# Stacked gate products in a recurrence, and attention scores in two steps per pair of heads

## The chip, the cores and the metric

The kernel runs on one core of one Trainium2 chip. The time is the device time of that core for one execution, in microseconds (us); a kernel's time is the median of its runs. TensorE is called PE in the profile, and its loading of the stationary operand PEld; DVE is VectorE, ACT is ScalarE, POOL is GpSimd, and SP is the engine that issues the DMAs.

## What is computed

One step of a 2-layer encoder, for a prompt of 512 tokens and a sample of 32 tokens, both with the same weights. Width is 1024. A layer is three parallel branches, a gated merge and a layer norm:

```python
def layer(x, pe, ...):                       # shortened
    u = x @ w_in                             # 1024 -> 8192 columns
    qa, ka, va, za, qb, kb, vb, zb, xr, zc, ga, gb, gc = split_cols(u)
    ya = band_attention(qa, ka, va, rel_table) * silu(za)      # 8 heads of 64
    yb = group_norm_heads(retention(rope(qb), rope(kb), vb)) * silu(zb)
    yc = rg_lru(xr, ...) * silu(zc)
    merged = sum(sigmoid(g) * (y @ w_branch[i]) for i, (g, y) in ...)
    r = ALPHA * x + merged @ w_out
    r = r + sigmoid(r @ w_ple_gate) * (pe @ w_ple)
    return layer_norm(r, ln_gain, ln_bias)

def rg_lru(xr, s_conv, s_lru, ...):          # shortened; w = 512 in 8 blocks of 64
    xc = conv_b + sum(xpad[:, j:j + t] * conv_w[j] for j in range(4))
    xb = xc.reshape(b, t, 8, 64)
    r = sigmoid(einsum('btni,nij->btnj', xb, w_gate_a) + b_gate_a)
    ig = sigmoid(einsum('btni,nij->btnj', xb, w_gate_x) + b_gate_x)
    log_a = -8.0 * r * softplus(-lru_lambda)
    a = exp(log_a);  bx = sqrt(-expm1(2 * log_a)) * ig * xc
    h = associative_scan(a, bx)              # h[t] = a[t] * h[t - 1] + bx[t]
```

The prompt's attention is over up to 512 keys in chunks of 64: a chunk of queries sees its own chunk and all before it. A learned bias per head is added to the scores ahead of the softmax. The sample's 32 queries see 256 cached keys and their own 32.

## The kernel before

**Layout.** Activations lie with features on the 128 partitions and the 544 tokens (512 and 32) along the free dimension. An fp32 product is made of three products of fp32r parts: each operand is cast to a high part (`hilo`, line 264, on ACT, for activations; `split`, line 211, on ACT, for weights), and DVE subtracts it to give the low part (lines 265 and 212). Products are high by high, high by low, and low by high.

**Blocks.** The weights are cut into blocks of 128 x 128. `block()` (line 256) makes six matmuls for one: three products, each for 288 and 256 tokens. Weights stream from DRAM in chunks of eight blocks (`load`, line 203, issued on SP), and are split four blocks at a time. Nearly all of PE's work is these blocks, and the rest of each layer is put between them.

**Order.** The order of the program is the order on every engine. It is written by hand: after each block `tick()` runs the jobs that are due. A job is a Python generator; what it yields is the number of ticks until it goes on, mostly an entry of the table `PACE`. A tick is thus one block, six matmuls.

**The recurrence's gates.** `lru_tile(t)` handles 128 of the 512 channels, two of the eight 64 x 64 gate blocks: convolution (lines 510 to 512), eight ticks (`lt1`), then cast and split of `xc` (547 columns: 512, three of padding, 32), five ticks (`lt2`), then two groups of six matmuls (line 522), three ticks (`lt3`) after each. A group is one gate for all 128 channels: its weight is block-diagonal, with two 64 x 64 blocks and zeros elsewhere, three products in two pieces of 274 columns, into two PSUM buffers (`sc` and `pv`). Three sigmoids on ACT follow a group (lines 525 to 527), and POOL multiplies the input gate by `xc` (lines 529, 530). `lru_job` then makes the coefficients and the scans (lines 555, 556).

**The attention.** For each pair of heads `attn_job` starts three steps of `attn_step`, eight ticks apart: query tiles 0 and 1 (128 and 256 keys), tile 2 (384), tile 3 (512). A step makes the scores of both heads (line 407, three products each, the two heads on the two halves of PE's rows), a softmax (lines 357 to 364, on DVE and ACT) and, at `at1` + `at1` + `at2` = 8 ticks after the scores, transposes of the probabilities (line 423) with their copies. The products with the values (line 441) wait in a list until the first transposes of the next pair's first step, where `flush()` makes them. `sample_job` does the same for the 32 sample tokens.

**PSUM** has eight banks: `mm` (two buffers of two banks) for blocks, `sc` (two), `tp` (one), `pv` (one). A `tmp` buffer is one of 14 in SBUF of 128 x 544 or a little more.

## Time and profile before

| | |
|---|---|
| time, median of 3 runs | 1309.05 us (1308.57 to 1309.22) |
| the profiled execution's own time | 1308.99 us |
| its span on the core | 1307.2 us |
| instructions in the span | 25,090 |
| mean granted clock of TensorE | 0.997 |
| PE, weight loads | busy 99% and 96% of the span |
| DVE, ACT, POOL | busy 55%, 42%, 13% of the span |

How to read the rows that follow in the prediction. A row of the timeline is: start in us from the span's start, duration in us, engine, line of the kernel, operation, output and inputs by the program's names, partitions x elements and type, number of instructions; then, in brackets, the idle time of the engine ahead of it and what ended it. PE rows overlap, since matmuls are pipelined: the distance of their starts is what one costs. A row of the waits is: engine, tile and line that waited, what released it, the sum of waiting in us, the count, the longest. In a row of the windows stand, for each stretch, its length, the busy time of PE, PEld, DVE, ACT, POOL and SP's DMA queue with counts, the granted clock, the share of the DMA engines and their GB/s.

### The profile page before, as it was taken

The numbers are of one execution on the slowest core, as the hardware profiler recorded it, in microseconds if no ns is written. First come the engines' busy times: TensorE is split into PE (matmuls) and PEld (weight loads), VectorE is DVE, ScalarE is ACT, GpSimd is POOL, SyncE is SP. The second block draws the span as 40 slices with busy tenths as digits, with TensorE's granted clock in tenths as the row PEclk, the third lists the DMA queues.
The fourth block names the chain that finished last, engine by engine and source line by source line (L and its number), as shares of the span: only waits on it lengthen the run. The fifth ranks groups of instructions, "written<-read, shape, count | busy, mean of one in ns | idle before, by whom it ended". The sixth has DMA issues, their size and how long they took to land.

```text
span 1307.2 us, 25090 instructions
## 1 busy us (share of the span) xinstructions
PE 1290.2 (99%) x10552; PEld 1255.8 (96%) x10552; DVE 719.6 (55%) x1273; ACT 547.0 (42%) x1083; POOL 176.3 (13%) x158
## 2 busy tenths in 40 slices
PE   9999999999999999999999999999999999999996
PEld 9999889999999999999989998999999999999996
DVE  5666663563754443455584756626637534434567
ACT  6665544323632233323277655443235322332231
POOL 0210121410101101000032102125001011010000
PEclk9999999999999999999999999999999999999998
DMA  7333522321222222434132335222212222224231
GB/s 285 132 131 98 174 66 83 96 92 51 96 81 82 98 80 82 165 101 143 65 112 72 130 99 166 74 83 89 87 62 81 98 81 89 90 82 166 81 114 69
DMA packets 44609, 134.80 MB, mean 103 GB/s; under 512 B 9488, under 2 KB 11792, under 8 KB 42704
## 3 DMA queue, kind: packets, MB, share of 16 engines
q1 hardware_dynamic: 44496, 133.20, 30.6%
q8 instruction: 83, 1.36, 0.5%
q14 instruction: 30, 0.25, 0.1%
HBM read 117.02 MB, written 11.70 MB: 98 GB/s over the span
## 4 chain that ended last, share of the span: by engine, by line
PE 95%; DVE 3%; DMA 1%; ACT 1%; issue 0%; SPq 0%; POOL 0%; DVEq 0%
PE mm L256 84%; PE sc L407 2%; PE pv L441 1%; PE tp L423 1%; PE tp L334 1%; DMA raw<-in_W 1%; PE sc L667 1%; PE pv L690 1%; PE pv L522 0%; DVE r L819 0%; PE sc L522 0%; DVE xl L265 0%; PE sc L750 0%; PE sc L603 0%; PE pv L685 0%; PE sc L494 0%
## 5 line engine op out<-in xcount | busy, mean ns | idle before, releaser
L256 PE MATMUL mm<-xh,wh 128*128 128x288 f32 x2144 | 455.5, 294 | 0.4 <-ACT xrp L900 0.4
L256 PE MATMUL mm<-xh,wl 128*128 128x288 f32 x2144 | 444.2, 288 | 0.0
L256 PE MATMUL mm<-xl,wh 128*128 128x288 f32 x2144 | 442.8, 288 | 0.0
L212 DVE TENSOR_TENSOR wl<-raw,wh 128x512 fp32r<-128x512 f32 (+1 forms) x354 | 262.6, 760 | 282.3 <-ACT wh L211 277.2
L256 PEld LDWEIGHTS mm<-xh,wh 128*128 128x128 f32 x2144 | 328.4, 189 | 10.8 <-issue 7.5
L256 PEld LDWEIGHTS mm<-xl,wh 128*128 128x128 f32 x2144 | 328.8, 188 | 0.0
L256 PEld LDWEIGHTS mm<-xh,wl 128*128 128x128 f32 x2144 | 328.6, 188 | 0.0
L211 ACT CAST wh<-raw 128x512 fp32r<-128x512 f32 (+1 forms) x354 | 208.2, 614 | 36.0 <-PE mm L256 30.8
L922 ACT ACTIVATE sg<-mm 128x544 f32<-128x544 f32 x48 | 30.0, 625 | 154.0 <-PE mm L256 154.0
L934 POOL TENSOR_TENSOR m<-m,sg 128x544 f32<-128x544 f32 x30 | 46.8, 1561 | 316.7 <-DVE sg L932 316.7
L359 ACT ACTIVATE sx<-sx,sst 128x128 f32<-128x128 f32 (+4 forms) x68 | 38.0, 559 | 67.1 <-DVE sst L357 60.2
L256 PE MATMUL mm<-xh,held 128*128 128x288 f32 (+1 forms) x320 | 64.1, 292 | 0.3 <-ACT ple L942 0.3
L256 PE MATMUL mm<-mh,wh 128*128 128x288 f32 (+1 forms) x256 | 53.0, 288 | 0.0
L256 PE MATMUL mm<-mh,wl 128*128 128x288 f32 (+1 forms) x256 | 53.0, 288 | 0.0
L256 PE MATMUL mm<-ml,wh 128*128 128x288 f32 (+1 forms) x256 | 52.8, 287 | 0.0
L256 PEld LDWEIGHTS mm<-xh,held 128*128 128x128 f32 x320 | 51.3, 188 | 0.6 <-ACT ple L942 0.5
L256 PE MATMUL mm<-xl,held 128*128 128x288 f32 (+1 forms) x160 | 46.4, 290 | 0.6 <-DVE xl L265 0.6
L264 ACT CAST xh<-r 128x544 fp32r<-128x544 f32 (+2 forms) x32 | 17.0, 532 | 68.3 <-DVE r L952 64.1
L932 DVE TENSOR_TENSOR sg<-mm,sg 128x544 f32<-128x544 f32 x32 | 23.2, 725 | 37.0 <-PE mm L256 37.0
L913 ACT ACTIVATE z<-mm 128x544 f32<-128x544 f32 x24 | 15.0, 626 | 60.6 <-PE mm L256 60.5
L571 POOL TENSOR_TENSOR swap<-swap,cst 128x544 f32<-128x544 f32 x16 | 24.9, 1554 | 108.3 <-DMA swap<-QB 32.1
L256 PEld LDWEIGHTS mm<-mh,wh 128*128 128x128 f32 x256 | 39.4, 189 | 0.0
(251 smaller groups left out, 1783.4 us busy)
## 6 DMA issues: line engine op xcount, KB each, us to landing
raw<-in_W SPq DMA_DIRECT2D x189, 512.0 KB, 3.3
pled<-ple SPq DMA_DIRECT2D x4, 1088.0 KB, 9.8
ple<-pled SPq DMA_DIRECT2D x4, 1088.0 KB, 7.0
bias<-in_RB SPq DMA_DIRECT2D x16, 256.0 KB, 3.7
x<-in_xT SPq DMA_DIRECT2D x4, 544.0 KB, 9.5
o_v<-VA SPq DMA_DIRECT2D x2, 1088.0 KB, 4.6
o_k<-KT SPq DMA_DIRECT2D x2, 1088.0 KB, 5.1
swap<-KB SPq DMA_DIRECT2D x32, 68.0 KB, 2.0
```

Source lines behind the costliest of these rows:

```text
L211: S.copy(h[:, k:k + step], t)
L212: V.tensor_tensor(lo[:, k:k + step], t, h[:, k:k + step].bitcast(F32), SUB)
L256: T.matmul(ps[:, MM0 + a:MM0 + b], lhsT=w[:, n % 4, :], rhs=x[:, a:b], start=first and i == 0, stop=last and i == 2)
L264: S.copy(h, src)
L334: T.transpose(tp[:rows, t * 128:(t + 1) * 128], src[:, t, c0:c0 + rows], ident)
L359: S.activation(x, x, AF.Exp, bias=s[:, 0:1], scale=-1.0, accum_out=s[:, 1:2])
L407: T.matmul(scs[j][:, o:o + n], lhsT=q_[r, p, i * 128:i * 128 + 128], rhs=k_[r, p, :n], start=k == 0, stop=k == 2)
L571: G.tensor_tensor(sw, sw, cst[:, C_SIN:C_SIN + N], MUL)
L913: S.activation(z, pv, AF.Sigmoid)
L922: S.activation(sg, pv, AF.Sigmoid)
L932: V.tensor_tensor(sg, pv, sg, MUL)
L934: (V if kind == "bB" and t == 7 else G).tensor_tensor(m, m, sg, ADD)
```

## The change

Two parts of the kernel are changed, with the paces that place them.

**Gate products.** After the split of `xc`, four DMAs within SBUF build two tiles `xs[0]` and `xs[1]` of 128 rows: the high part of one gate block's 64 channels in one half of the rows, and the low part of the same channels in the other. The weight tile holds the `a` and the `x` matrix of that block side by side, and the same again below. A group is now one gate block: two products instead of three (high weights by the stacked rows, low weights by the stacked rows), and the result has gate `a` on 64 partitions and gate `x` on the other 64. So a tile has two groups of four matmuls. The first group uses the two `sc` buffers, the second `pv` and `tp`. Four sigmoids on 64 partitions follow each group, of 274 and 273 columns. POOL multiplies all 547 columns in one instruction. The tiles `lru_r`, `lru_i`, `lru_a` are 547 wide. The stacked rows also add the product of low weights by low activations to the sum. `lt0`, the delay ahead of a tile's job, is now 2, 11, 12, 13 for the four tiles (before: 2, and 8 for tile 1).

**Scores.** A pair of heads has a wide step (query tiles 3 and 1: 512 and 256 keys, in `sc`, `sc`, `tp`, `pv`) and a narrow one (tiles 2 and 0: 384 and 128 keys side by side in the two `sc` buffers); 11 ticks follow the first, 13 the second. The list of value products is emptied after the first transposes of the wide step. `sample_job` loads its bias later, makes the scores of both halves in one go, and all its transposes in one go into two `sc` buffers. The copies of VA from PSUM go from ACT to DVE.

```diff
@@ -69,8 +69,8 @@
 PACE = {
     "turn": 2, "spill": 16, "tk": 1, "bc0": 3, "bc1": 4, "x": 5,
-    "va0": 5, "va": 3, "step": 8, "attn_end": 9, "at1": 3, "at2": 2, "at3": 3, "sample": 11, "sa1": 4, "sa2": 4,
-    "sa3": 3, "lt0": 2, "lt00": 8, "lt1": 8, "lt2": 5, "lt3": 3, "lru0": 3, "lru1": 3, "lru2": 1, "lru3": 3,
+    "va0": 5, "va": 3, "step": (11, 13), "attn_end": 3, "at1": 3, "at2": 2, "at3": 3, "sample": 14, "sa1": 4, "sa2": 4,
+    "sa3": 3, "lt0": (2, 11, 12, 13), "lt1": 8, "lt2": 5, "lt3": 3, "lru0": 2, "lru1": 2, "lru2": 1, "lru3": 2,
     "rope1": 6, "rope2": 5, "rope3": 3, "tok": 2, "kv": 4, "mu": 2, "mu2": 2, "dec": 2, "rs": 2, "y1": 3,
     "y2": 1, "y3": 1, "gn": 8, "gn1": 2, "gn2": 6, "gn3": 2}
@@ -377,11 +378,11 @@
                 for j in range(2):
                     G.memset(env["bias", p, j][0:64, 448:512], NEG)
-                for qs in ((0, 1), (2,), (3,)):
-                    if qs[0] == 2 and p < 3:
+                for n, qs in enumerate(((3, 1), (2, 0))):
+                    if n and p < 3:
                         bias_loads(p + 1)
                     add(attn_step(p, qs))
-                    yield PACE["step"]
+                    yield PACE["step"][n]
             yield PACE["attn_end"]
             flush()
@@ -393,22 +394,31 @@
         def attn_step(p, qs):
             QTh, QTl, KTh, KTl = (env[k] for k in ("QTh", "QTl", "KTh", "KTl"))
-            scs, xs, todo = [psum("sc") for _ in range(2)], [], []
-            o = 0
+
+            wide = qs[0] == 3
+            scs, xs = [psum("sc") for _ in range(2)], [tmp("sx", (128, 512)) for _ in range(2)]
+            at_ = {(qs[0], j): (scs[j], xs[j], 0) for j in range(2)}
+            if wide:
+                x = tmp("sx", (128, 512))
+                at_.update({(qs[1], j): (psum(("tp", "pv")[j]), x, 256 * j) for j in range(2)})
+            else:
+                at_.update({(qs[1], j): (scs[j], xs[j], 128 * (qs[0] + 1)) for j in range(2)})
             now = [], []
 
-            for j in range(2):
-                xs.append(tmp("sx", (128, 512)))
             for i in qs:
                 n = (i + 1) * 128
...
                     for j in range(2):
                         r = slice(64 * j, 64 * j + 64)
-                        T.matmul(scs[j][:, o:o + n], lhsT=q_[r, p, i * 128:i * 128 + 128], rhs=k_[r, p, :n],
+                        sc, x, o = at_[i, j]
+                        o *= not wide
+                        T.matmul(sc[:, o:o + n], lhsT=q_[r, p, i * 128:i * 128 + 128], rhs=k_[r, p, :n],
                                  start=k == 0, stop=k == 2)
                 for j in range(2):
-                    now[j].append((xs[j][:, o:o + n], scs[j][:, o:o + n], env["bias", p, j][:, 512 - n:]))
-                o += n
+                    sc, x, o = at_[i, j]
+                    c = 0 if wide else o
+                    now[j].append((x[:, o:o + n], sc[:, c:c + n], env["bias", p, j][:, 512 - n:]))
+            todo = []
             for j in range(2):
                 for a in todo:
@@ -417,21 +427,21 @@
                 norm(*a)
             yield PACE["at2"]
-            for j in range(2):
+            for x in xs + ([at_[1, 0][1]] if wide else []):
                 tp = psum("tp")
-                for c in range(0, o, 128):
-                    T.transpose(tp[:, c:c + 128], xs[j][:, c:c + 128], ident)
-
-                if j == 0 and qs[0] == 0:
+                mine = sorted((o, i, j) for (i, j), (_, y, o) in at_.items() if y is x)
+                end = mine[-1][0] + 128 * (mine[-1][1] + 1)
+                for c in range(0, end, 128):
+                    T.transpose(tp[:, c:c + 128], x[:, c:c + 128], ident)
+
+                if wide and x is xs[0]:
                     flush()
-                c = 0
-                for i in qs:
+                for c, i, j in mine:
                     copy("p%d" % j)(env["PT"][j][:, :i + 1, i * 128:i * 128 + 128],
                                     tp[:, c:c + 128 * (i + 1)].rearrange("p (a b) -> p a b", b=128))
-                    c += 128 * (i + 1)
+                if not wide and x is xs[1]:
+                    env["pvs"].append(lambda: attn_pv(p))
                 yield PACE["at3"]
-            if qs[-1] == 3:
-                env["pvs"].append(lambda: attn_pv(p))
 
         def attn_pv(p):
@@ -453,37 +463,39 @@
         def sample_job():
             ks, vc = sample_loads()
+            while "ya" not in env:
+                yield 2
+            yield PACE["sample"]
             sb = [tmp("sb", (128, PAST + NS)) for _ in range(2)]
             for h in range(8):
                 Q.dma_start(out=sb[h % 2][32 * (h // 2):32 * (h // 2) + 32],
                             in_=RB[l, h, 0:NS, 128:128 + PAST + NS])
-            while "ya" not in env:
-                yield 2
-            yield PACE["sample"]
+            yield 12
             xs = []
+            scs = [psum("sc") for _ in range(2)]
             for j in range(2):
                 r = slice(64 * j, 64 * j + 64)
-                sc = psum("sc")
                 for p in range(4):
-                    T.matmul(sc[32 * p:32 * p + 32, :PAST + NS], lhsT=env["qs"][r, p], rhs=ks[r, p],
+                    T.matmul(scs[j][32 * p:32 * p + 32, :PAST + NS], lhsT=env["qs"][r, p], rhs=ks[r, p],
                              tile_position=(64 * j, 32 * p))
+            for j, sc in enumerate(scs):
                 xs.append(exps(tmp("sx", (128, PAST + NS)), sc[:, :PAST + NS], sb[j]))
                 yield PACE["sa1"]
...
                 norm(*x)
             yield PACE["sa2"]
...
@@ -503,7 +516,7 @@
         def lru_tile(t):
             if t == 0:
-                env["lru"] = [sl("lru_r"), sl("lru_i"), sl("lru_a")]
+                env["lru"] = [sl(k, shape=(128, 4, W547)) for k in ("lru_r", "lru_i", "lru_a")]
...
@@ -511,23 +524,28 @@
                 V.scalar_tensor_tensor(xc, xrp[:, t, j:j + W547], pcol(P_CW + 4 * j, t), xc, MUL, ADD)
             yield PACE["lt1"]
-            xch, xcl = (tp_.tile([128, W547], F32R, tag="tmp", name="xch") for _ in range(2))
+
+            xch, xcl, *xs = (tp_.tile([128, W547], F32R, tag="tmp", name="xhl") for _ in range(4))
+            rows = slice(0, 64), slice(64, 128)
             hilo(xch, xcl, xc)
+            for b in range(2):
+                Q.dma_start(out=xs[b][rows[b]].bitcast(F32), in_=xch[rows[b]].bitcast(F32))
+                Q.dma_start(out=xs[b][rows[1 - b]].bitcast(F32), in_=xcl[rows[b]].bitcast(F32))
             yield PACE["lt2"]
-            for g in range(2):
-                w, lo = ([parts[(l * NB + AT["wg"] + g * 4 + t) // 4][i][:, t] for i in range(2)])
-                ps = psum("sc"), psum("pv")
-                for i, (wg, x) in enumerate(((w, xch), (w, xcl), (lo, xch))):
+            for b in range(2):
+                n = l * NB + AT["wg"] + 2 * t + b
+                ps = [psum(k) for k in (("pv", "tp") if b else ("sc", "sc"))]
+                for i in range(2):
                     for p_, c0 in ((ps[0], 0), (ps[1], W547 - 274)):
-                        T.matmul(p_[:, :274], lhsT=wg, rhs=x[:, c0:c0 + 274], start=i == 0, stop=i == 2)
-                d = (I if g else R)[:, t]
-                b_ = pcol(P_BX if g else P_BA, t)
-                S.activation(d[:, :274], ps[0][:, :274], AF.Sigmoid, bias=b_)
-                S.activation(d[:, 274:NP], ps[1][:, 1:NP - 273], AF.Sigmoid, bias=b_)
-                S.activation(d[:, NP:], ps[1][:, 274 - NS:274], AF.Sigmoid, bias=b_)
+                        T.matmul(p_[:, :274], lhsT=parts[n // 4][i][:, n % 4], rhs=xs[b][:, c0:c0 + 274],
+                                 start=i == 0, stop=i == 1)
+
+                for d, r, b_ in ((R, rows[b], P_BA), (I, rows[1 - b], P_BXS)):
+                    b_ = pcol(b_, t)[r]
+                    S.activation(d[rows[b], t, :274], ps[0][r, :274], AF.Sigmoid, bias=b_)
+                    S.activation(d[rows[b], t, 274:], ps[1][r, 1:274], AF.Sigmoid, bias=b_)
                 yield PACE["lt3"]
-            G.tensor_tensor(I[:, t, :NP], I[:, t, :NP], xc[:, :NP], MUL)
-            G.tensor_tensor(I[:, t, NP:], I[:, t, NP:], xc[:, NP + 3:], MUL)
+            G.tensor_tensor(I[:, t], I[:, t], xc, MUL)
             if t == 3:
                 env["gates"] = True
@@ -901,7 +919,7 @@
                     Q.dma_start(out=o_cv[l, :, :, 0:3], in_=xrp[:, :, NP:NP + 3])
                     Q.dma_start(out=o_cv[l, :, :, 3:6], in_=xrp[:, :, NP + NS + 3:NP + NS + 6])
-                add(lru_tile(t), PACE["lt00"] if t == 1 else PACE["lt0"])
+                add(lru_tile(t), PACE["lt0"][t])
@@ -1085,10 +1103,8 @@ (on the host, before the launch)
         for n, (kind, t, k) in enumerate(BLOCKS):
             if kind == "wg":
-                W[l, n // 8, :, n % 8] = 0
-                for b in range(2):
-                    r = slice(64 * b, 64 * b + 64)
-                    W[l, n // 8, r, n % 8, r] = g["w_gate_x" if k // 4 else "w_gate_a"][l, 2 * (k % 4) + b]
+                ax = [g[a][l, k] for a in ("w_gate_a", "w_gate_x")]
+                W[l, n // 8, :, n % 8] = np.tile(np.concatenate(ax[::-1] if k % 2 else ax, 1), (2, 1))
```

The places in the program where this moves work, on the engines that wait or are waited for there:

ACT, layer 0 of before, from the last group of tile 0 (gate `x`) to the first group of tile 1; `par_91` are the layer's biases and other columns, `xrp` is the padded input of the convolution, and the convolution's step is tile 2's:

```order
L211 CAST wh<-raw 128x512
L525 ACTIVATE lru_i<-sc,par_91 128x274
L526 ACTIVATE lru_i<-pv,par_91 128x238
L527 ACTIVATE lru_i<-pv,par_91 128x32
L264 CAST xch<-xc 128x547
L510 ACTIVATE xc<-xrp,par_91 128x547
L211 CAST wh<-raw 128x512
L525 ACTIVATE lru_r<-sc,par_91 128x274
```

The same stretch in the changed kernel:

```order
L212 CAST wh<-raw 128x512
L545 ACTIVATE lru_r<-pv,par_91 64x274
L546 ACTIVATE lru_r<-tp,par_91 64x273
L545 ACTIVATE lru_i<-pv,par_91 64x274
L546 ACTIVATE lru_i<-tp,par_91 64x273
L265 CAST xhl<-xc 128x547
L523 ACTIVATE xc<-xrp,par_91 128x547
L212 CAST wh<-raw 128x512
L545 ACTIVATE lru_r<-sc,par_91 64x274
```

The cast of a tile stands directly behind the sigmoids of the last group of the tile before, in both. There are four of them, on 64 partitions, where there were three on 128.

SP, the same stage of before, where only weights, two small outputs and the second chunk of `ple` are issued:

```order
L850 DMA pled<-ple 128x2176
L203 DMA raw<-in_W 128x1024 x2
L902 DMA o_cv<-xrp 512x1x3
L903 DMA o_cv<-xrp 512x1x3
L203 DMA raw<-in_W 128x1024 x4
```

SP after; `xhl<-xhl` is one copy of 64 rows into `xs`:

```order
L868 DMA pled<-ple 128x2176
L204 DMA raw<-in_W 128x1024
L532 DMA xhl<-xhl 64x547
L533 DMA xhl<-xhl 64x547
L532 DMA xhl<-xhl 64x547
L533 DMA xhl<-xhl 64x547
L204 DMA raw<-in_W 128x1024
L920 DMA o_cv<-xrp 512x1x3
L921 DMA o_cv<-xrp 512x1x3
L532 DMA xhl<-xhl 64x547
```

Four copies a tile are added to SP's queue, sixteen a layer, between the loads of weights.

DVE, layer 0, the softmax of the first attention step of before, from its first reductions to its first normalisation (`sst` holds the row sums; ISA is the reduction of line 357, which also adds the bias):

```order
L357 ISA sx,sst<-sc,bias 128x128
L357 ISA sst 128x1
L357 ISA sx,sst<-sc,bias 128x256
L357 ISA sst 128x1
L555 SCALAR_TENSOR_TENSOR lru_i<-lru_a,lru_r 128x512
L556 SCALAR_TENSOR_TENSOR lru_i<-lru_a,par_91,lru_r 128x32
L212 TENSOR_TENSOR wl<-raw,wh 128x512
L363 RECIPROCAL sst<-sst 128x1
L364 TENSOR_SCALAR sx<-sx,sst 128x128
```

The same after (the scans are lines 573 and 574, the reduction is line 358):

```order
L358 ISA sx,sst<-sc,bias 128x512
L358 ISA sst 128x1
L358 ISA sx,sst<-tp,bias 128x256
L358 ISA sst 128x1
L573 SCALAR_TENSOR_TENSOR lru_i<-lru_a,lru_r 128x512
L574 SCALAR_TENSOR_TENSOR lru_i<-lru_a,par_91,lru_r 128x32
L213 TENSOR_TENSOR wl<-raw,wh 128x512
L573 SCALAR_TENSOR_TENSOR lru_i<-lru_a,lru_r 128x512
L574 SCALAR_TENSOR_TENSOR lru_i<-lru_a,par_91,lru_r 128x32
L364 RECIPROCAL sst<-sst 128x1
L365 TENSOR_SCALAR sx<-sx,sst 128x512
```

Between the step's first reductions and its first normalisation there are now two scans where there was one (a further pair stands ahead of the reductions), and the reductions are over 512 and 256 keys, in the place of 128 and 256.

28 lines of the change are left out of this document (15 added, 13 removed).

## Prediction

> **What bounds the kernel now.** I read the page first (busy shares, slices, chain), then the waits of the engines, then the timeline of the two stages that change.
>
> ```profile
> PE 1290.2 (99%) x10552; PEld 1255.8 (96%) x10552; DVE 719.6 (55%) x1273; ACT 547.0 (42%) x1083; POOL 176.3 (13%) x158
> PEclk9999999999999999999999999999999999999998
> PE 95%; DVE 3%; DMA 1%; ACT 1%; issue 0%; SPq 0%; POOL 0%; DVEq 0%
> ```
> ```profile
> PE tp L750 <- DVE r L968: 2.0, 2, 1.4
> SPq L203 <- DVE wl L212: 787.4, 139, 11.0
> ```
> PE is the chain for 95% of the span, and its longest entry in the list of waits is 2.0 us in all. So PE is a queue that hardly ever stops: what is taken out of it is gained in full, and every wait put into it is lost in full, since nothing later in the program has room to make it good. Everything below is therefore priced on PE alone; the other engines count only where PE waits for them. The second row says that the weight loads stand on SP until a buffer is free (787.4 us of waiting): they are early, and more work on SP costs nothing until that is used up.
>
> **The recurrence's products.** A tile now has two groups of six products; it gets two groups of four. The order has 32 matmuls of 274 columns fewer, and nothing else of PE's changes here.
>
> ```profile
> 37.91 0.64 ACT L211 CAST wh<-raw 128x512 fp32r<-128x512 f32 x1
> ...
> 39.39 0.69 DVE L212 TENSOR_TENSOR wl<-raw,wh 128x512 fp32r<-128x512 f32 x1
> 40.26 0.72 DVE L265 TENSOR_TENSOR xch<-xc,xch 128x547 fp32r<-128x547 f32 x1
> 41.56 0.19 PEld L522 LDWEIGHTS sc<-xch,held 128*128 128x128 f32 x1
> 41.68 0.29 PE L522 MATMUL sc<-xch,held 128*128 128x274 f32 x1
> ...
> 42.31 0.29 PE L522 MATMUL pv<-xch,held 128*128 128x274 f32 x1
> 42.51 0.49 ACT L525 ACTIVATE lru_r<-sc,par 128x274 f32<-128x274 f32 x1 [0.67 <-PE sc L522]
> 42.90 0.45 ACT L526 ACTIVATE lru_r<-pv,par 128x238 f32<-128x238 f32 x1
> ...
> 46.44 0.66 ACT L264 CAST xch<-xc 128x547 fp32r<-128x547 f32 x1
> 46.46 1.30 POOL L529 TENSOR_TENSOR lru_i<-lru_i,xc 128x512 f32<-128x512 f32 x1 [46.02 <-ACT lru_i L526]
> 47.13 1.21 DVE L265 TENSOR_TENSOR xch<-xc,xch 128x547 fp32r<-128x547 f32 x1 [1.06 <-ACT xch L264]
> ```
> ```profile
> 42.60 2.27 PE mm L256 x18
> ```
> ```profile
>   ACT lru_r L527: 0.6, 2
> ```
> Six products start between 41.68 and 42.31, one every 0.126 us; the blocks between them have the same pitch (2.27 over 18). 32 x 0.126 = 4.0 us gained. Line 522's matmuls also waited 0.6 us for the sigmoids of the group before (last row, from that line's own view); with four PSUM buffers for two groups that goes: 0.6 gained.
>
> **The transfers** are what I expect to decide. Before, the operands of a group were ready when DVE had split them (line 265). Now four DMAs follow the split, and PE still comes five ticks after it (a tick is one block, six matmuls, 0.755 us). What a small copy within SBUF costs:
>
> ```profile
> DMA to landing us min/median/max: 1.9/2.0/3.7
> L568 SPq DMA_DIRECT2D swap<-KB x16: 582/588/591, 146.0 to 824.1; - x16
> ```
> ```profile
> o_y<-tk SPq DMA_DIRECT2D x6, 256.0 KB, 2.1
> ```
> The rope's swaps (68 KB) land 2.0 us after their issue, the 256 KB of o_y 2.1; a copy of 64 rows has 140 KB, so I take 2.1, and 0.1 for the two semaphores (issue and wake). Each issue holds SP for 0.59, but only the first two copies, of which one goes out while DVE still splits, are needed by the first group; the other two have three ticks more.
>
> [...]
>
> Tile 0, layer 0: in the order its split no longer stands behind the next tile's convolution, only behind a weight's cast and split (0.69 from about 38.55, the end of the cast at 37.91) and small steps, so it ends at about 40.25 instead of 40.98. 40.25 + 2.2 = 42.45 against 41.56, when PE's weight load came: PE waits 0.9. Layer 1:
>
> ```profile
> 687.77 0.72 DVE L265 TENSOR_TENSOR xch<-xc,xch 128x547 fp32r<-128x547 f32 x1
> ...
> 690.14 0.19 PEld L522 LDWEIGHTS sc<-xch,held 128*128 128x128 f32 x1
> ```
> 688.49 + 2.2 = 690.7 against 690.14: 0.55.
>
> Tiles 1 to 3: the order puts the cast of a tile on ACT right behind the sigmoids of the last group of the tile before, and on PE there are 36 block matmuls between that group and the next tile's first. With P the start of that last group: its fourth product starts at P+0.38, the first sigmoid 0.20 later (42.31 to 42.51), four sigmoids at 0.39 each (42.51 to 42.90) end their turn at P+2.14, the cast (0.66) at P+2.80. POOL starts its product at the last sigmoid's end, P+2.25, for about 1.36. The split beside a POOL product took 1.21 instead of 0.72 (47.13), ending 0.58 after POOL's (46.46 + 1.30 to 48.34): P+4.2. Plus 2.2: P+6.4. PE is there at P + 0.50 + 36 x 0.126 - 0.12 = P+4.9. Wait 1.45 for tiles 1 and 2. For tile 3 a weight's cast and split (0.69) go ahead of both: 2.15.
>
> Sum: 0.9 + 0.55 + 4 x 1.45 + 2 x 2.15 = 11.55 us lost. Low end: copies at 1.9, splits undisturbed (0.65 less) and nothing ahead in tile 3: 6.7. High end: the slowest landing of the row, 3.7, in tile 3 of both layers and 2.3 elsewhere: 17.
>
> **The attention's scores.** The 24 row-tiled matmuls of a pair of heads stay, but in two visits a pair of heads instead of three.
>
> ```profile
> 94.69 0.41 PE L256 MATMUL mm<-xh,wl 128*128 128x288 f32 x2
> 95.03 0.33 PE L407 MATMUL sc<-KTh,QTh 64*128 64x128 f32 x2
> ...
> 95.42 0.34 PE L407 MATMUL sc<-KTh,QTh 64*128 64x256 f32 x2
> ...
> 95.92 0.52 PE L256 MATMUL mm<-xh,wh 128*128 128x288 f32 x2
> 96.28 0.41 PE L256 MATMUL mm<-xl,wh 128*128 128x288 f32 x2
> ```
> ```profile
> 110.27 0.50 PE L407 MATMUL sc<-KTh,QTh 64*128 64x512 f32 x2
> 110.61 0.39 PE L407 MATMUL sc<-KTh,QTl 64*128 64x512 f32 x2
> 110.84 0.40 PE L407 MATMUL sc<-KTl,QTh 64*128 64x512 f32 x2
> 111.17 0.52 PE L256 MATMUL mm<-xh,wh 128*128 128x288 f32 x2
> ```
> ```profile
> 128.35 0.44 PE L407 MATMUL sc<-KTh,QTh 64*128 64x384 f32 x2
> ...
> 129.07 0.52 PE L256 MATMUL mm<-xh,wh 128*128 128x288 f32 x2
> ```
> A pair of block matmuls takes 0.25. The pair ahead of a score step takes 0.34, the pair after it 0.36: a visit costs 0.20 besides its own work. That work is 0.89 (128 and 256 keys), 0.72 (384) and 0.90 (512), and leaving costs 0.10 of it (the third pair at 512 takes 0.33, the second 0.23). The wide step (512, then 256): 0.90 - 0.10 + 0.50 = 1.30; the narrow one (384, then 128): 0.72 - 0.09 + 0.39 + 0.09 = 1.11; together 2.41 against 2.51. With one visit less, 0.30 a pair, 2.4 in eight. The twenty transposes stay twenty. Against it: in six pairs the pending PV products stood between transposes and scores; now blocks follow them, one visit more each: 1.2 lost. The sample's scores come in one group instead of two: 0.2 a layer, 0.4 gained; bounds 0 and twice that.
>
> **The first wide step.** There DVE runs late, and its order changes.
>
> ```profile
> 97.14 0.28 DVE L357 CUSTOM_DVE_ANT_0 sx<-sc,bias 128x128 f32<-128x128 f32 x1
> ...
> 97.70 1.22 DVE L555 TENSOR_TENSOR_SCAN lru_i<-lru_a,lru_r 128x512 f32<-128x512 f32 x1
> ...
> 99.35 1.86 DVE L212 TENSOR_TENSOR wl<-raw,wh 128x512 fp32r<-128x512 f32 x1 [0.25 <-ACT wh L211]
> ...
> 101.32 0.29 DVE L364 TENSOR_SCALAR sx<-sx,sst 128x128 f32<-128x128 f32 x1
> ```
> Before, the first transposes, eight ticks after the scores, found their rows normalised at 101.61, half a microsecond early. Now two scans more (1.22 and a short one each, some 1.45) stand ahead of that step, and its first softmax has 512 keys instead of 128 (0.4 by the widths). The split at 99.35, held up by POOL (1.86 instead of 0.69), may lose 1.2. 2.9 + 0.4 - 0.5 - 0.4 (the longer visit) = 2.4 late, or 1.2 without POOL in the way: 2.0 a layer, 4.0 lost. Bounds: 0, and twice that if POOL holds the scans too. Later wide steps I put at nothing: eight ticks of blocks cover their two more reductions; uncovered, about 1 us each.
>
> At nothing also: the copies of VA on DVE (covered by eight ticks of blocks until their buffer is used again; without that, 0.7 each); 32 more issues on SP (19 us, out of the 787 of waiting); the sample's eight bias loads, now ahead of a rope tile's swaps: 4.7 + 2.4 + 2.0 = 9.1 us against eleven ticks, 8.3, so up to 0.8 of DVE a layer, in the range.
>
> **Sum** against the profiled execution, 1308.99 (span 1307.2; the median of the three runs is 1309.05, 0.06 above): - 4.0 - 0.6 + 11.55 - 2.4 + 1.2 - 0.4 + 4.0 = + 9.35, so 1318.3 us.
>
> **Rivals.**
> Faster: the copies land before PE comes and the first wide step finds DVE early. 1308.99 - 6.2 = 1302.8. For it: the five ticks that cover the copies are 3.8 us and a copy lands in 2.0, so cast and split may use 1.8. Against it: the cast cannot start before the sigmoids of the group before, 2.14 us after P, and 2.0 of landing alone is 40% of the 4.9 that there are. It decides if all new waits together stay under 3.6 us. 0.15.
> Same: the low end of the transfers and no wait in the first step: 1308.99 - 6.2 + 6.7 = 1309.5. 0.12.
> Slower than forecast: DVE is late in every wide step, 6 x 1.0, and the first ones cost 4 each: 1318.3 + 10 = 1328. For it: the two more reductions; against: DVE is busy for 55% only. 0.13.
> The clock falls in the waits.
>
> ```profile
> 655.00:668.00 13.00, 11.30 (x89) 10.85 (x88) 11.63 (x24) 10.31 (x22) 8.79 (x11) 1.00 0.00 0
> 1290.00:1307.00 17.00, 5.92 (x47) 5.25 (x46) 12.68 (x26) 0.77 (x2) 1.13 (x1) 0.76 0.36 132
> ```
> With 1.7 us of idle in 13 the granted clock stays 1.00; it is 0.76 only where PE has 11 of 17 idle. Waits of 2 us are like the first row. If four waits did halve it for about 4 us each, 8 us more: 1326. 0.03. [...]
>
> **How the numbers follow.** The forecast has 0.57, with its own range 1313 to 1324. A change under 0.2% (2.6 us) cannot be told from none. Faster 0.15, same 0.12, slower 0.73. The range, 1303 to 1328, leaves out about half of the first rival and some of the third and fourth.
>
> **What would show it.** Right: PE waits for DMA at the first group of each recurrence tile, least in tile 0, most in tile 3, 5 to 6 us a layer; score visits of 1.3 and 1.1 us; PE waiting once a layer, for DVE, at the first transposes. Wrong: no DMA among PE's releasers in the recurrence, which would mean that a copy of 64 rows lands far below 2 us or that ACT casts earlier than its order allows; or waits at all wide steps.

## The result, and the profile after

The changed kernel takes 1356.82 us (median of 4 runs, 1355.34 to 1357.91), the kernel before 1308.89: a ratio of 1.0368 (95% interval 1.0352 to 1.0383), 48 us slower. The forecast was 1318.3 with a range up to 1328: right in sign, wrong by a factor of five in size. The profiled execution took 1355.34 us, its span is 1353.6. The page's engine row and clock row, and PE's own list of waits (engine, tile, line, releaser: us in all, times, longest):

```profile
PE 1300.6 (96%) x10520; PEld 1266.3 (94%) x10520; DVE 719.9 (53%) x1281; ACT 550.6 (41%) x1087; POOL 173.7 (13%) x150
PEclk9998999999999999999999899999999999999998
```
```profile
PE sc L540 <- DMA xhl<-xhl: 18.4, 8, 4.5
PE tp L435 <- DVE sx L365: 8.0, 2, 4.2
PE sc L494 <- DVE sst L358: 5.6, 2, 3.0
...
PE mm L257 <- ACT wh L212: 1.8, 2, 0.9
```

PE's list of waits sums to 43.6 us, before to 7.6. The first three rows are 32.0 of the 36.0 that came in. And PE is busy for 10 us longer with 32 matmuls fewer: part of the time its clock is half. The windows of the changed kernel around tile 3 (length, busy time of PE, PEld, DVE, ACT, POOL with counts, granted clock, DMA share, GB/s) show both:

```profile
72.00:76.00 4.00, 0.06 (x1) 0.00 (x0) 0.82 (x2) 0.00 (x0) 0.00 (x0) 1.00 0.96 265
76.00:79.60 3.60, 3.55 (x17) 3.58 (x18) 0.48 (x1) 2.34 (x5) 0.00 (x0) 0.59 0.01 2
79.60:83.00 3.40, 3.40 (x27) 3.40 (x27) 0.21 (x1) 1.96 (x5) 0.19 (x1) 0.94 0.44 154
```

PE is idle for 4 us while the DMA engines are 96% busy. Then come 3.6 us in which PE is busy almost without a break, but does 17 matmuls in the place of 28, at a granted clock of 0.59. There are eight such stretches; by the starts of consecutive block matmuls they cost 0.8 to 1.9 us each, 10.8 in all.

Both kernels make the same 9,024 block matmuls in the same order, so the difference of their start times tells where time was lost. Per layer, in us, from the profiled execution of each run (blocks counted from the layer's start; the total is at the last block of the program):

| kernel | recurrence (40-92) | first pair (104-128) | next pairs (128-168) | sample, last pair (168-216) | retention (216-368) | total |
|---|---|---|---|---|---|---|
| changed, layer 0 / 1 | 10.8 / 12.1 | 8.5 / 7.5 | -1.6 / -1.7 | 4.2 / 4.8 | 1.4 / 1.4 | 46.4 |
| e1_rec_only | 12.0 / 12.9 | 7.4 / 6.2 | 0 / 0 | 0 / 0 | 0 / 0 | 36.9 |
| e2_att_only | 0 / 0 | 1.0 / 1.1 | -1.6 / -1.7 | 2.9 / 4.2 | 1.4 / 1.4 | 8.3 |
| e3_copies_early | 2.8 / 2.0 | 8.2 / 7.3 | -1.6 / -1.7 | 2.9 / 2.9 | 1.4 / 1.4 | 24.5 |
| e7_attn_later | 9.5 / 11.8 | 1.9 / 2.1 | -4.2 / -4.2 | 8.0 / 8.5 | 1.3 / 1.4 | 35.2 |
| t1_all | -1.9 / -1.1 | 5.3 / 6.5 | -5.3 / -5.2 | 5.3 / 9.1 | 0.9 / 0.9 | 14.0 |
| t5_att_rope | 0 / 0 | 1.6 / 1.1 | -1.6 / -1.7 | 1.7 / 1.7 | 0.9 / 0.9 | 3.0 |
| t7_rec_va | -2.4 / -0.8 | 3.2 / 4.6 | 0 / 0 | 0 / 0 | 0 / 0 | 5.6 |

A stage's number also holds the work that was moved across its borders. In the changed kernel, blocks 128 to 168 have 352 PE instructions between them where they had 367, and blocks 168 to 216 have 462 where they had 451: most of the -1.6 is work that now stands later.

### The profile page after: what moved, and what is told of

The parts are those of the page before. It is cut to its first block, busy times and chain, and to the rows that moved or that the text cites. A ratio compares the mean times of both kernels' runs of the same rounds, so it can differ in the third digit from the quotient of the medians.

```text
span 1353.6 us, 25118 instructions
## 1 busy us (share of the span) xinstructions
PE 1300.6 (96%) x10520; PEld 1266.3 (94%) x10520; DVE 719.9 (53%) x1281; ACT 550.6 (41%) x1087; POOL 173.7 (13%) x150
## 5 line engine op out<-in xcount | busy, mean ns | idle before, releaser
L213 DVE TENSOR_TENSOR wl<-raw,wh 128x512 fp32r<-128x512 f32 (+1 forms) x354 | 267.7, 773 | 309.2 <-ACT wh L212 308.4
L257 PEld LDWEIGHTS mm<-xh,wh 128*128 128x128 f32 x2144 | 333.0, 191 | 6.8 <-issue 2.8
L257 PEld LDWEIGHTS mm<-xh,wl 128*128 128x128 f32 x2144 | 332.1, 190 | 2.7 <-DVE wl L213 2.7
L257 PEld LDWEIGHTS mm<-xl,wh 128*128 128x128 f32 x2144 | 333.3, 190 | 0.0
L360 ACT ACTIVATE sx<-sx,sst 128x512 f32<-128x512 f32 (+2 forms) x68 | 37.7, 557 | 51.9 <-DVE sst L358 40.5
L440 ACT COPY PT<-tp 128x384 f32<-128x384 f32 (+2 forms) x64 | 24.9, 428 | 44.8 <-PE tp L435 38.0
## 6 DMA issues: line engine op xcount, KB each, us to landing
xhl<-xhl SPq DMA_DIRECT2D x32, 136.8 KB, 2.5
```

Of the source, the lines that this page charges most:

```text
L213: V.tensor_tensor(lo[:, k:k + step], t, h[:, k:k + step].bitcast(F32), SUB)
L257: T.matmul(ps[:, MM0 + a:MM0 + b], lhsT=w[:, n % 4, :], rhs=x[:, a:b], start=first and i == 0, stop=last and i == 2)
L360: S.activation(x, x, AF.Exp, bias=s[:, 0:1], scale=-1.0, accum_out=s[:, 1:2])
L440: copy("p%d" % j)(env["PT"][j][:, :i + 1, i * 128:i * 128 + 128], tp[:, c:c + 128 * (i + 1)].rearrange("p (a b) -> p a b", b=128))
```

## The experiments

### One part at a time, and the clock by itself

e1_rec_only and e2_att_only are the two halves of the change, each with its own paces; the copies of VA on DVE belong to e2. e3_copies_early is one line of the changed kernel, e4_clock_probe a job in the kernel before:

```diff
-"lt1": 8, "lt2": 5                       # e3
+"lt1": 5, "lt2": 8
+def probe():                             # e4, from layer 0's first za on
+    for n in range(3, 17):
+        ps, x = psum("sc"), tmp("probe", (128, 512))
+        T.transpose(ps[:, :128], cst[:, C_ID:C_ID + 128], ident)
+        for _ in range(n): S.copy(x[:, :128], ps[:, :128])
+        ps = psum("sc"); T.transpose(ps[:, :128], x[:, :128], ident)
+        yield 18
```

> The kernel before with the recurrence's part alone (stacked products, copies, four PSUM buffers, its paces); attention, sample and VA as before. Theory W (waits): the loss of 48 us is made of PE waits at separate places, and each wait of more than about 2.6 us is followed by some 3 us in which the granted clock is half. Then this kernel has the recurrence's share of the comparison by blocks, 11.1 and 12.4 us in the two layers, and a part of the first attention step's (8.4 and 7.5 in the changed kernel), since the recurrence's second half now runs 12 ticks later, into that step: 1309 + 23.5 + 6 = 1338 us, 1332 to 1348. Theory I (interplay): the recurrence loses only because the attention's new steps hold DVE, POOL and the queues: then 1309 to 1318.

> The kernel before with the attention's part alone (wide and narrow steps, the sample's new order, VA's copies on DVE, the paces of the steps). Theory W: the middle of the attention gains 9.2 us in two layers, the sample's transposes lose 14.4 (they wait for the two sc buffers that the fourth wide step holds), and the first wide step loses little, since the recurrence's scans are done earlier: 1309 - 9 + 14 + 2 = 1316 us, 1312 to 1322. Theory I, by which the loss at the first step and the sample is the wide step's own DVE work and not the late recurrence: 1309 - 9 + 14 + 16 = 1330.

> The changed kernel with lt1 8 -> 5 and lt2 5 -> 8: cast, split and copies go out three ticks (2.3 us) earlier, and every group of products stays at its place. Theory W: waits of 0.94, 2.7, 1.4, 4.0 us a layer become 0, 0.4, 0, 1.7 or less, none is long enough for the clock, so the recurrence goes from +23.5 us to between -4 and +2, and the total to 1357 - 25 = 1332 us, 1328 to 1338. Rival M: the clock falls because of the stacked matmuls themselves and not after idle time; then only the waits go, 13 us, and the half clock stays: 1344.

> The kernel before with fourteen waits of PE put into the merge of layer 0, 18 blocks apart, where PE does nothing but blocks: a transpose, n copies of 128x128 on ACT (n = 3 to 16), a transpose that needs the last. The waits grow from about 1 to about 4 us. Theory W: below some length between 1.5 and 2.7 us the blocks after a wait keep their pitch of 0.126 us, above it the pitch is about 0.24 for 2.5 to 4 us, so each long wait costs itself and about half of that again. Rival M: pitch stays 0.126 after all of them, since nothing but idle time was added. The total is then 1309 + the sum of waits (about 35) + 0 by M, or + 10 to 15 more by W.

e1 took 1349.6 us (ratio 1.0308, 1.0293 to 1.0323), just above its range; e2 1317.6 (1.0070, 1.0053 to 1.0087) and e3 1335.3 (1.0209, 1.0185 to 1.0232), both inside the range of theory W. In their parts they fit less well, so that e2's total is in part luck: the sample lost 7.1 us of the 14 expected, the middle gained 3.3 of the 9, and the retention lost 2.8 that I had not expected; e3's recurrence is still 4.8 us behind, where between -4 and +2 was expected, since two waits of 2.5 and 3.7 us for copies are left. The halves add: 41 and 9 against 48. By the table the first pair's loss comes with the recurrence (7.4 in e1, 1.0 in e2), the sample's with the attention. Theory I falls: the recurrence loses as much without the attention's new steps. e1's list of waits:

```profile
PE sc L528 <- DMA xhl<-xhl: 18.4, 8, 4.2
PE tp L424 <- DVE sx L365: 8.3, 2, 4.2
PE tp L335 <- ACT vatok L336: 4.4, 2, 2.2
```

The third row is a wait for the copies of VA, which e1 leaves on ACT. In the changed kernel, with these copies on DVE, it is 0.6 us in all: this move was worth some 1.9 us a layer, and hid part of what the recurrence costs.

The probe took 1383.4 us (one run). Its waits came out longer than meant (52.9 us in all), and the half clock followed ten of fourteen: waits of 1.84, 2.19, 2.73, 2.88 us and all from 4.8 on, but not those of 0.95, 2.18, 2.49, 3.03. So it isn't the length of the wait. The ends of the ten slow stretches lie on one grid with a period of 3.413 us. Cut on that grid, the windows of the probe (columns as above) sort themselves:

```profile
401.63:405.04 3.41, 1.57 (x14) 1.32 (x12) 0.69 (x1) 2.56 (x8) 0.00 (x0) 1.00 0.35 114
405.04:408.45 3.41, 3.41 (x18) 3.41 (x17) 1.37 (x3) 0.62 (x1) 0.56 (x1) 0.50 0.10 40
418.69:422.10 3.41, 1.22 (x11) 0.98 (x10) 1.19 (x1) 1.86 (x7) 0.64 (x1) 1.00 0.41 156
422.10:425.51 3.41, 3.41 (x15) 3.41 (x16) 0.00 (x0) 0.00 (x0) 0.00 (x0) 0.50 0.02 5
435.75:439.16 3.41, 1.84 (x15) 1.59 (x13) 0.69 (x1) 2.46 (x7) 0.00 (x0) 1.00 0.03 10
439.16:442.57 3.41, 2.49 (x20) 2.50 (x21) 0.62 (x1) 1.94 (x5) 0.00 (x0) 1.00 0.00 0
473.28:476.69 3.41, 1.64 (x13) 1.64 (x14) 0.00 (x0) 2.09 (x8) 0.00 (x0) 1.00 0.41 154
476.69:480.10 3.41, 3.41 (x29) 3.41 (x28) 3.09 (x3) 0.61 (x1) 1.74 (x1) 1.00 0.00 0
```

In this run a window at full clock with PE busy for 1.57 us or less is followed by one at 0.50; with 1.64 or more the next stays at 1.00. A wait of 2.2 us that straddles a border costs nothing more, one of 1.84 inside a window costs another 1.5. Rival M falls: idle time alone does it. In the changed kernel's trace the eight slow stretches are one or two times 3.413 us long, and start 7, 19, 42, 197, 203, 216 and 239 times 3.413 us after the first. On that grid the windows at full clock with PE busy for 1.42 us or less are followed by one at 0.50, the next two, with 1.99 and 2.02, by one at 1.00. The other traces with slow stretches, each laid on its own grid, show the same with a less sharp border: together, all 70 windows at full clock with PE busy for 1.53 us or less are followed by half clock, and none of the 132 from 1.95 to 2.8. Of the 33 between, eight are, and all eight hold transposes or other small matmuls beside the blocks. PE need not be idle for a whole window: 1.57 us busy of 3.41 (46%) were followed by half clock in the probe.

### What makes a copy late

Of the 32 copies in the changed kernel, 13 had nothing but copies of their own tile in flight when they were issued: these landed 2.24 to 2.53 us later (median 2.39). The other 19, with a load or an output in flight, took 2.38 to 4.30 (median 3.76), and none landed before the transfer that was ahead of it; the earliest came 0.17 us after. What is in flight at issue isn't the whole price in every run: in t1_all three copies of layer 1, issued from 705.39 on, took 3.95 to 4.44 us with only copies of their own tile ahead of them. The trace has an instruction fetch in that stretch; whether it is the cause was not tested. Tile 3's timeline of the changed kernel:

```profile
70.98 0.33 SPq L204 DMA_DIRECT2D raw<-in_W  x1
71.41 0.47 SPq L532 DMA_DIRECT2D xhl<-xhl  x1
71.97 0.55 SPq L533 DMA_DIRECT2D xhl<-xhl  x1
...
76.05 0.79 PE L540 MATMUL sc<-xhl,held 128*128 128x274 f32 x4 [3.99 <-DMA xhl<-xhl]
```

The load of 512 KB landed at 74.67, the copies at 75.33 and 75.92. Two single edits of the changed kernel: the o_cv outputs moved from ahead of tile 1's copies to behind tile 3's groups (e5), and the copies issued by POOL (e6).

```diff
-        Q.dma_start(out=o_cv[l, :, :, 0:3], in_=xrp[:, :, NP:NP + 3])      # e5: both o_cv lines,
+    if t == 3:                                                             # now at lru_tile's end
+        env["gates"] = True; Q.dma_start(out=o_cv[l, :, :, 0:3], in_=xrp[:, :, NP:NP + 3])
-    Q.dma_start(out=xs[b][rows[b]]...)                                     # e6: all four
+    G.dma_start(out=xs[b][rows[b]]...)
```

> The changed kernel with its two o_cv outputs (6 KB each in pieces of 12 bytes, landing 3 to 6 us after issue) issued behind the last recurrence tile and not ahead of tile 1's copies. Theory F (first in, first out): a copy lands right behind the transfer that was issued ahead of it on the queue; the second o_cv lands at 52.64 and 723.21 us, the first copy of tile 1 at 52.81 and 723.49, though it was issued 4 us earlier. With o_cv gone tile 1's copies land 2.3 us after issue, PE's wait there falls from 2.7 to about 1.3 us, too short for the clock, and with it go 1.5 us of half speed: 1357 - 2 x 2.7 = 1351.5 us, 1349 to 1354. Rival B (bandwidth or the split on DVE): the landing of 4 us is that of a copy in a busy stage, and nothing changes: 1357.

> The changed kernel with the four copies of a tile issued from POOL's queue, where no weight and no output stands. Theory F: they pass the loads, and land in 2.3 to 2.8 us at every tile, tile 3 too (3.9 to 4.3 before): the waits become 0.9, 1.3, 1.4, 2.0 us, the half clock in this stage goes: 1357 - 2 x 7 = 1343 us, 1338 to 1348; the time that POOL takes for an issue is not known here, and could add up to 1 us to each wait. Rival B: the landings at tiles 1 and 3 stay near 4 us, as the same sixteen engines move the same bytes: 1353 to 1360.

e5: 1354.85 us (1.0353, 1.0337 to 1.0368). Tile 1's first copies now land 2.26 and 2.42 us after issue (4.04 and 4.06 before), and PE waits 1.91 and 1.92 there in the place of 2.71 and 2.70:

```profile
48.94 0.46 SPq L532 DMA_DIRECT2D xhl<-xhl  x1
50.31 0.46 SPq L533 DMA_DIRECT2D xhl<-xhl  x1
...
52.72 0.75 PE L540 MATMUL sc<-xhl,held 128*128 128x274 f32 x4 [1.91 <-DMA xhl<-xhl]
```

So a transfer ahead delays the copy. The time moved less than I expected (2.0 against 5.3 us, above the range, and hardly clear of the scatter): the second copy is issued only after a split that takes 1.34 us beside POOL, so PE still waits 1.9, and in layer 1 the half clock stays. e6: 1352.4 us (1.0337, 1.0320 to 1.0354), between the two ranges and nearer to rival B: from another queue the first two copies of tile 3 still landed 4.6 to 4.9 us after issue, the first at 76.11 where SP's load landed at 75.54. So it is not the order of SP's queue. From 72 to 76 us the DMA engines are 99% busy in e6; what holds the copies there was not shown.

### The first pair and the sample

e7 moves the first attention step, e8 the sample's paces, in the changed kernel:

```diff
-            yield 4                       # e7, in attn_job ahead of the pairs' loop
+            yield 16
-"sample": 14, "sa1": 4, "sa2": 4, "sa3": 3        # e8
+"sample": 13, "sa1": 2, "sa2": 2, "sa3": 8
```

> The changed kernel with the first attention step 12 ticks later (yield 4 -> 16 ahead of the pairs' loop), so that the scans and POOL's products of the recurrence, which now end later, are done before it. Theory P (pile-up): PE's wait at the first transposes, 4.2 and 3.8 us, and the half clock after it are owed to the scans, and to DVE's instructions beside POOL's products (1.74 to 1.90 us in the place of 0.7); both go: 1357 - 15 = 1342 us, 1339 to 1347. Rival H (heavy): the wide step's softmax over 512 and 256 keys doesn't fit into eight ticks by itself: the wait stays at 2 us or more: 1350 to 1358.

> The changed kernel with the sample's paces 14, 4, 4, 3 -> 13, 2, 2, 8: its transposes come two blocks ahead of the fourth wide step and not five behind it, its value products when that step's scores have been read. Theory S: PE waited 2.6 and 3.0 us because the transposes need both sc buffers while the wide step holds them; 5.6 us of waits and 2 to 3 us of half speed go, and at most 1 us comes back at the wide step, which now waits for the sample's copies: 1357 - 7 = 1350 us, 1347 to 1353. Rival D: DVE is late there anyway (1.31 and 1.44 us for a normalisation beside POOL's rope products), and the wait moves to the wide step's transposes: 1355 to 1358.

e7: 1344.6 us (1.0281, 1.0265 to 1.0296), theory P. The timeline of the changed kernel at its first wide step shows what piled up there:

```profile
102.44 5.22 POOL L571 TENSOR_TENSOR lru_r<-lru_r,lru_i 128x547 f32<-128x547 f32 x3 [18.26 <-ACT lru_r L568]
102.78 1.90 DVE L266 TENSOR_TENSOR KTl<-KT,KTh 128x544 fp32r<-128x544 f32 x1
104.71 3.50 DVE L213 TENSOR_TENSOR wl<-raw,wh 128x512 fp32r<-128x512 f32 x2
...
113.84 2.27 POOL L571 TENSOR_TENSOR lru_r<-lru_r,lru_i 128x547 f32<-128x547 f32 x1
114.90 1.30 DVE L574 TENSOR_TENSOR_SCAN lru_i<-lru_a,par,lru_r 128x32 f32<-128x32 f32 x1
...
118.72 1.12 PE L435 MATMUL tp<-cst,sx 128*128 128x128 f32 x4 [4.23 <-DVE sx L365]
```

Three POOL products take three of DVE's operations from 0.7 to 1.75-1.90 us, a fourth takes a short scan from 0.26 to 1.30; 4.3 us of DVE in all. Before, the first three of these products were made six to seven blocks earlier, and the scans up to six. The recurrence's tiles now stand nine ticks apart, its second half starts 11 ticks later, and falls into the first attention step. The 512 keys of the wide step are not what costs: e1, with the old step behind the late recurrence, waits 4.2 and 4.1 us at the same place, and e2, with the wide step behind the old recurrence, has no wait for DVE there.

e8: 1353.65 us (1.0345, 1.0330 to 1.0360), between the two theories: PE still waited 2.2 us a layer at the transposes, now for their own normalisation (1.63 us beside POOL for 288 columns). In the changed kernel the same place reads:

```profile
192.44 1.76 POOL L594 TENSOR_TENSOR KB<-KB,cst 128x512 f32<-128x512 f32 x1 [3.71 <-DVE KB L591]
193.17 1.31 DVE L365 TENSOR_SCALAR sx<-sx,sst 128x512 f32<-128x512 f32 x1
...
194.56 1.32 POOL L589 TENSOR_TENSOR swap<-swap,cst 128x544 f32<-128x544 f32 x1
194.59 1.44 DVE L365 TENSOR_SCALAR sx<-sx,sst 128x256 f32<-128x256 f32 x1
...
196.70 1.04 PE L494 MATMUL sc<-cst,sx 128*32 128x128 f32 x4 [2.60 <-DVE sst L358]
```

Two normalisations of 0.49 and 0.35 us (their times without POOL beside them) take 1.31 and 1.44. Behind them stand the reductions of the fourth wide step, and PE goes on when these have read the `sc` buffers that the transposes need.

### Taking the waits away

t1_all puts the edits together, t2_rec and t3_att are the halves with them (in t2 the old sample's pace also goes from 11 to 21; t3 has the edit of the buffer alone):

```diff
-"lt0": (2, 11, 12, 13), "lt2": 5         # t1, t2; o_cv as in e5; first step: yield 14
+"lt0": (2, 7, 8, 9), "lt2": 9
-            tps = psum("sc"), psum("sc")  # t1, t3
+            tps = psum("sc"), psum("tp")
-"sa1": 4, "sa2": 4, "sa3": 3             # t1
+"sa1": 2, "sa2": 4, "sa3": 4
```

> The changed kernel with its three waits taken away: lt0 (2, 11, 12, 13) -> (2, 7, 8, 9) and lt2 5 -> 9 (cast, split and copies four ticks ahead of where they were, groups of tiles 1 to 3 at their places), o_cv behind the last tile, the first attention step 10 ticks later, the sample's second transposed tile in tp and not in sc, and its paces 4, 4, 3 -> 2, 4, 4. Theory W+F: the matmuls saved are all that is left, 32 x 0.126 = 4 us, 0.6 for line 522's old waits, 1 to 2 for the score visits, and up to 3.5 of small waits for weights stay: 1303 us, 1301 to 1308. Rival L (a cost of the stacked form that the waits hid, such as DVE and ACT work or the weights' order): 1309 or more though no long wait is left.

> The kernel before with the recurrence's part alone, the same lt0 and lt2, o_cv behind the last tile, and the old attention's first step 10 ticks later (the sample with it). Against e1_rec_only (1349.6) it tells what the stacked products are worth when their copies have nine ticks: theory W+F: 1309 - 4.6 = 1304.5, 1303 to 1309. Rival L: 1310 to 1316.

> The kernel before with the attention's part alone, as in e2_att_only (1317.6), but the sample's second transposed tile in tp, which the wide step's first reductions have released, in the place of the second sc buffer. Theory S: the waits of 2.6 us a layer and the half clock after one of them go: 1317.6 - 5.2 - 1 = 1311.4, 1310 to 1313; the score visits' gain of 2.4 us is then offset by the flush apart from the scores (1.2), the wait at the first wide step (about 1 a layer) and the weights' late split in the retention (0.9 a layer). Rival D: DVE is late there anyway and the wait moves on: 1315 to 1318.

t1: 1320.7 us (1.0097, 1.0081 to 1.0113), 36 of the 48 us back, but 12 short. The recurrence gains 1.9 and 1.1 us, with all copies in time but one (0.5). The rest of the loss is again waits, at other places: 5.8 us at transposes for DVE, 2.5 at the sample's scores. That fits neither side of the expectation, which had long waits gone. t2: 1326.25 (1.0135, 1.0120 to 1.0150), above both of its ranges: the recurrence breaks even, with 2.2 us a layer of it lost to the wait for VA's copies, as in e1, and the old attention, moved by ten ticks, waits at its transposes (8.2 us in all) and loses 7 more in the retention, which I didn't follow up. t3: 1318.0 (1.0069, 1.0051 to 1.0086), as e2: another PSUM buffer only moved the wait, 1.8 us a layer, to the value products. Theory S falls as a way to gain time: the buffer is what PE waits for in the changed kernel, but freeing it hands the wait on.

Then the tiles six ticks apart, so that the recurrence ends no later (t4), rope's products on DVE (t5), and both (t6):

```diff
-"lt0": (2, 11, 12, 13), "lt2": 5         # t4, t6; o_cv as in e5
+"lt0": (2, 8, 6, 4), "lt2": 8
-            G.tensor_tensor(sw, sw, cst[:, C_SIN:C_SIN + N], MUL)     # t5, t6; the two of KB too
+            V.tensor_tensor(sw, sw, cst[:, C_SIN:C_SIN + N], MUL)
```

> The kernel before with the recurrence's part alone, its tiles six ticks apart and not nine (lt0 (2, 8, 6, 4)), lt2 8, o_cv behind the last tile; the attention stands where it was. The recurrence then ends 6 ticks earlier than in the changed kernel, about where it ended before. Theory P (late recurrence): with copies hidden and the recurrence not late, only the matmuls saved are left: 1309 - 4.6 + up to 2 = 1305 us, 1303 to 1309. Rival L (the stacked form costs by itself: eight sigmoids of 0.39 us a tile on ACT where there were six of 1.13 us in sum for a group): ACT falls behind in this stage, and PE waits for casts, copies or vatok (2.2 us a layer in e1_rec_only): 1311 to 1320.

> e2_att_only (1317.6) with the three products of a rope tile on DVE and not on POOL. Theory D: the sample's transposes are late because DVE's normalisations and reductions beside POOL's rope products take 1.3 to 1.6 us in the place of 0.35 to 0.7; without POOL beside them DVE is in time, though it has 1.5 us more work a tile: the wait of 2.6 us a layer and the half clock go, 1311 us, 1309 to 1313. Theory S (the two sc buffers are held until the wide step's second reduction, wherever DVE stands): the wait stays above 1.5 us: 1315 to 1319.

> The changed kernel with both edits, the recurrence's tiles six ticks apart (lt0 (2, 8, 6, 4), lt2 8, o_cv behind the last tile) and rope's products on DVE. Theories P and D together: no wait above 1.5 us is left in the recurrence, at the first wide step and at the sample: 1357 - 28 - 14 - 8 = 1307 us, 1304 to 1312. If the first wide step still waits for DVE (its scans and softmax stand closer than in the kernel before): 1312 to 1322.

t5: 1312.06 us (1.0028, 1.0017 to 1.0039), theory D: with POOL out of the way the sample's stage costs 1.7 us a layer in the place of 2.9 and 4.2, and no half clock. The wait doesn't go, though: 1.4 us a layer stay, with the same releaser as in e2 (the reduction that reads the `sc` buffer). t4: 1318.9 (1.0081, 1.0066 to 1.0096), rival L, by PE's list of waits:

```profile
PE sc L528 <- DMA xhl<-xhl: 4.5, 2, 3.0
PE tp L335 <- ACT vatok L336: 4.4, 2, 2.2
PE tp L424 <- DVE sx L365: 2.2, 2, 1.5
```

Packed tighter, the tiles leave the copies of tile 2 behind a load. The second row is the wait for VA's copies on ACT, the same 2.2 us a layer as in e1 and t2. t6: 1323.85 (1.0118, 1.0101 to 1.0135), above both of its ranges, and the sum of the two losses within 2 us. The last two take these waits one by one:

```diff
-"lt2": 8                                  # t7: lt2 10, VA's copies on DVE, and the first
+"lt2": 10                                 # pair's bias loaded when attn_job starts
-                G.tensor_tensor(R[:, t], R[:, t], I[:, t], MUL)       # t8, on top of t7
+                V.tensor_tensor(R[:, t], R[:, t], I[:, t], MUL)
```

> t4_rec_tight (1318.9) with three things that its waits point to: two ticks more for the copies (lt2 8 -> 10; tile 2 waited 3.0 and 1.5 us behind a weight's load), VA's copies on DVE (2.2 us a layer of waiting for vatok, which ACT copied late), and the first pair's bias loaded as soon as its attention job exists (DVE waited 1.2 us for it). Theory: the stacked products are worth their 4.6 us where copies, ACT and the first softmax are all in time: 1309 - 4.6 + about 2 = 1306, 1303 to 1310. Rival L: a stage that is full on ACT, DVE and SP's queue hands the wait on each time, to vatok or to the first transposes: 1311 to 1317.

> t7_rec_va with the four products of the recurrence's scan inputs (lru_r x lru_i) on DVE and not on POOL, where each held up a split of DVE by about 1.1 us. If what is left at the first transposes is DVE beside POOL: 1 to 3 us less than t7_rec_va. If DVE is short of time by itself: the same or up to 2 us more.

t7: 1316.25 us (1.0058, 1.0046 to 1.0071); t8: 1316.6 (1.0063, 1.0049 to 1.0076), the same. t7's list of waits:

```profile
PE tp L424 <- DVE sx L365: 5.1, 2, 2.6
...
PE sc L528 <- DMA xhl<-xhl: 1.3, 1, 1.3
...
PE tp L335 <- ACT vatok L336: 1.0, 2, 0.5
```

The recurrence gains 2.4 and 0.8 us, and the wait at the first transposes takes back more. Moving POOL's products to DVE doesn't help there. By its expectation DVE would then be short of time by itself, but the run doesn't show it: in t7 the products hold up four of DVE's operations by 1.0 to 1.2 us each, in t8 their own four times 0.70 us stand on DVE instead, and in both DVE is idle for 1.2 us right ahead of the first normalisation, waiting for a weight's cast on ACT (t7, then t8):

```profile
102.30 0.69 DVE L213 TENSOR_TENSOR wl<-raw,wh 128x512 fp32r<-128x512 f32 x1 [1.21 <-ACT wh L212]
```
```profile
102.05 0.69 DVE L213 TENSOR_TENSOR wl<-raw,wh 128x512 fp32r<-128x512 f32 x1 [1.22 <-ACT wh L212]
```

What makes this step late in t7 is open between the scans, the weights' splits and ACT's casts. No version that I ran beats the kernel before; whether another table of paces would is open.

## Why the prediction was wrong, point by point

By stages the forecast was +7.0 us for the recurrence, +4.0 for the first pair and -1.6 for the rest of the attention. By the table it is +22.9, +16.0 and +8.5.

- **PE as a queue that loses every wait in full**: right, and too mild. The step that failed is the one on the clock: I took one row with 1.7 us of idle in 13 for the shape of every wait, and gave the half clock 0.03. In the traces it goes by the busy time of a window of 3.41 us: 0.50 after each of the 70 with 1.53 us or less. It cost 10.8 us in the blocks alone.
- **The products**: right. t7's layer 0, with no wait in this stage, gains 2.4 us there, where 2.3 a layer was forecast.
- **The transfers decide**: right; the term was mis-sized: 11.55 forecast, 18.4 measured. By tiles (layer 0 / 1): tile 0 0.9 / 0.55 forecast, 0.94 / 0.76 measured; tile 1 1.45, 2.71 / 2.70; tile 2 1.45, 1.39 / 1.42; tile 3 2.15, 3.99 / 4.46. Where nothing else was in flight, at tile 2, cast, split, POOL and copy came out as priced. A free copy was priced at 2.2 (2.1 by the rows, 0.1 for the semaphores as an estimate) and measured 2.39 to its landing; in tile 1 of layer 0 the second copy was issued 0.03 after the split's end, and PE's first product started 0.13 after it landed. I priced every copy as a free one, and kept the row's slowest landing, 3.7, for the range of tile 3 alone. I had noted where the loads and o_cv stand in SP's order, and called the queue free because SP had 787 us of waiting; what is in flight when the copy is issued was the price. The term's bounds, 6.7 and 17, don't come out of what they name either (4.7 and 16.0); 18.4 lies outside both. The 2.3 of the high end comes from none of the prediction's rows, and no run shows it as the price of every copy: with nothing else in flight the copies took 2.24 to 2.53, the others 2.38 to 4.30.
- **The first wide step**: place right, mechanism in part. Forecast 2.0 a layer, measured waits of 4.2 and 3.8, and 8.5 and 7.5 with the clock. The scans and POOL are what makes DVE late, as I had it, but the 0.4 for the wider softmax is not it (e1 waits as long with the old step), and I didn't see that the recurrence ends 11 ticks later. My upper bound was for POOL holding the scans too; in layer 0 POOL held three other operations and a short scan.
- **The score visits**: forecast -2.4 with 1.2 back, and 0.4 for the sample: 0.8 a layer in all. Right in size: over blocks 104 to 376, without PE's waits, e2's layer 0 is 0.8 us shorter than before, and t5's layers are 1.1 and 0.9. The -1.6 in the table is not this gain but mostly moved work. The retention's 1.4 a layer was in no term; 0.9 of it is a wait for a weight's cast on ACT, at block products behind the attention.
- **The sample at -0.4**: failed. I priced its visits, not the order in which it stands to POOL's rope products and to the fourth wide step; 5.6 us of waits and two slow stretches.
- **Later wide steps at nothing**: right; no wait of more than 0.3 us there. **VA's copies at nothing**: too low a worth; left on ACT they cost 2.2 us a layer (e1).
- **Rivals**: "slower, DVE late in all wide steps" has the sign, not the mechanism. The clock's rival had the mechanism with the wrong trigger. The sum of several rivals together, which happened, was in no case. That the sign came out right is no support for the sum: its two largest terms were both too small.

## What to carry to other kernels

Where PE never stops, price a DMA that is put in front of it by what is in flight when it is issued, not by its own landing: in the changed kernel the copies took 2.39 us alone and 3.76 behind a transfer (medians), and the 19 behind one landed 0.17 us after it at the earliest. Lay the grid of these traces, 3.41 us, over every wait of more than about 1.8 us (the shortest with half clock after it in the probe was 1.84), and add up to half of a window, 1.7 us, an estimate from the clock of 0.50, for each window that leaves PE busy for 1.53 us or less (here the slow stretches, two of them two windows long, cost 0.8 to 1.9 each). Where the grid stands differs from trace to trace: its first border is 1.5 us after the span's start in the changed kernel's, 1.9 in that of before, 2.3 in the probe's. So for waits between about 1.8 and 3.4 us this is a chance and not a certainty: in the probe half clock followed 1.84, 2.19, 2.73 and 2.88, but not 2.18, 2.49 and 3.03. A stage that is moved later is to be followed to its end: here the recurrence's second half ran into the next stage's softmax, and cost as much there as its copies did at home.
